# Two layers of a hybrid encoder trunk on one core: where the activation's hi and lo parts start in SBUF, relative to the weights'

## The chip, the cores and the metric

The kernel runs on one core of one Trainium2 chip. The time is device microseconds of one execution; the verdict compares medians of repeated runs of the kernel before and the kernel after on the same chip.

## The reference

Two layers on x of shape (1, 256, 1024), in float32. Each has three sub-layers of the form x <- LayerNorm(alpha x + f(x)): a SwiGLU feed-forward network (FFN) of width 2816, a mixer, and a second FFN.

```python
for l in range(DEPTH):
    x = _layernorm(DEEPNORM_ALPHA * x + FFN_RES * _swiglu(x, ffn1_w_in[l], ffn1_w_out[l]), ln1_g[l], ln1_b[l])
    mix = _hybrid_mixer(x, l, w_mix_in[l], ...)
    x = _layernorm(DEEPNORM_ALPHA * x + mix, ln2_g[l], ln2_b[l])
    x = _layernorm(DEEPNORM_ALPHA * x + FFN_RES * _swiglu(x, ffn2_w_in[l], ffn2_w_out[l]), ln3_g[l], ln3_b[l])
```

The mixer multiplies the normalised stream h with one wide input projection, whose columns feed three branches and their gates: A, differential attention; B, a chunked state-space scan (SSD) behind a short convolution; C, stick-breaking attention. Each branch's output is projected to 1024 columns, multiplied by its sigmoid gate, and summed, and one output projection follows.

## The kernel before

**Products in three passes.** Every float32 factor of the large products is split into a high part (rounded to the matmul's float32r) and a low part (the rest): on ScalarE the cast at line 91 writes `whi`, on VectorE the subtraction at line 92 writes `wlo`. For activations `split_act` (lines 126 and 127) does the same. A product is hi x hi, then two cross terms: three matmuls (`passes`).

**Weights.** They come from HBM in blocks of 1 MB through the SP queue into `raw` (two buffers, line 105), are split in halves of 128 x 1024 into `whi` and `wlo` (six buffers each), and are used once. TensorE gives the buffers back.

**Activations.** The stream x (256 tokens in two tiles of 128, t = 0 and 1) is kept transposed as `xT`: `xThi` and `xTlo`, each 8 slices (k) of 256 columns, so 8192 bytes of a partition. There are two ways of using it:
- *xT streamed.* `gemm_s` (line 133): the weights' 128 x 128 piece is stationary, 256 columns of `b[:, k, :]` stream. It serves the FFN's gate and up products (`part_s`), most of the mixer's projections (`block_s`) and the branch projections (`proj`, where b is the branch's output oA, oB or oC). A block of 256 weight columns is 2 x 8 x 3 = 48 matmuls.
- *xT stationary.* `block_a` (line 362, 512 weight columns stream) in the mixer and `part_a` (line 269, 256 columns) for the first tile of an FFN.

The FFN's middle parts `hhi` and `hlo` are stationary at line 302, under 512 streamed columns of the output weights: `whi`/`wlo`, or, for the last three tiles, `dhi`/`dlo`, which are kept until the LayerNorm of t = 0 is under way. The mixer's `mT` is stationary at line 724.

**Order.** The matmuls' order on TensorE is that of the program's planner; the order within a block is written out. At the end of a sub-layer the LayerNorm of t = 0 runs while the held matmuls of t = 1 go on, and the transposes (line 143) and `split_act` of each t build the next xT. In the mixer the scan's decay matrices come back through a DMA (line 457) to VectorE (line 489), ScalarE (line 493) and VectorE again (line 494), and line 500's matmuls use them.

**Where things lie.** A buffer starts where the one before it in its pool ends, rounded up to 32 bytes; pools stand one behind another, and the FFN's and the mixer's pool start at the same place. Counted from the declared sizes, in bytes modulo 512: `ident` 128, `xt`, `xThi`, `xTlo`, `raw`, `whi` and `wlo` 96; all large tiles of the FFN 288 (gb, sq, rawo, hhi, hlo, h, dhi, dlo); the mixer's slots 288, up to `cbm` at 352, and `t10` and `q3` at 384. The branch outputs use slots: oA in t6 and t7 (hi, lo), oB in t9 and t10, oC and later mT in t1 and t3.

Of the kernel before, what the change touches and what calls it, by code (L numbers as in the profile page):

```python
# [11 lines left out]
F32 = mybir.dt.float32  # L12
F32R = mybir.dt.float32r
# [7 lines left out]
P = 128  # L21
D = 1024
S = 256
L = 2
FF = 2816
KT = D // P
NT = S // P
EPS = 1e-5
ALPHA = (2 * L) ** 0.25
LAG = 2  # L30
HOLD = 3
OFF_QA, OFF_KA, OFF_VA, OFF_ZB, OFF_XBC, OFF_DTB, OFF_QC, OFF_KC, OFF_VC, OFF_G = (
    0, 1024, 2048, 3072, 4096, 5632, 5648, 6672, 7696, 8720)
NEG = -float(2 ** 100)
# [4 lines left out]
def hybrid_trunk(ctx: ExitStack, tc: tile.TileContext, x, ffn1_w_in, ffn1_w_out, ln1_g, ln1_b,  # L39
# [6 lines left out]
    const = ctx.enter_context(tc.tile_pool(name="const", bufs=1))  # L46
    keep = ctx.enter_context(tc.tile_pool(name="keep", bufs=1))
    wraw = ctx.enter_context(tc.tile_pool(name="wraw", bufs=2))
    wsp = ctx.enter_context(tc.tile_pool(name="wsp", bufs=6))
    sm = ctx.enter_context(tc.tile_pool(name="sm", bufs=2))  # L50
# [21 lines left out]

    ident = const.tile([P, P], F32, name="ident")
    make_identity(nc, ident)
    half_neg = const.tile([P, 8], F32, name="half_neg")
    dve.memset(half_neg, -0.5)


# [39 lines left out]
    def load_rows(w, k0, dst=None, raw=None):  # L118
        with tc.issue_after(dma[0]):
            return load(w, k0, 2, 0, 1024, dst, None, raw)  # L120
# [24 lines left out]
            split_act(xT[0][:, 4 * q:4 * q + 4, t * P:(t + 1) * P], xT[1][:, 4 * q:4 * q + 4, t * P:(t + 1) * P], pv)  # L145

    def new_xT():
        return (keep.tile([P, KT, S], F32R, name="xThi"), keep.tile([P, KT, S], F32R, name="xTlo"))

    def layernorm(t, accs, coef, gb, sq):  # L150
        st = sm.tile([P, 5], F32, name="st")
        for h in range(2):
            yh = xt[:, t, h * 512:(h + 1) * 512]
            dve.scalar_tensor_tensor(out=yh, in0=accs[h], scalar=coef / ALPHA, in1=yh, op0=ALU.mult, op1=ALU.add,  # L154
                                     accum_out=st[:, h:h + 1])
        dve.tensor_scalar(out=st[:, 4:5], in0=st[:, 0:1], scalar1=st[:, 1:2], scalar2=-1.0 / (D * math.sqrt(D)),
                          op0=ALU.add, op1=ALU.mult)
        dve.tensor_scalar(out=st[:, 2:3], in0=st[:, 0:1], scalar1=st[:, 1:2], scalar2=-1.0 / D, op0=ALU.add, op1=ALU.mult)
        act.activation(out=sq, in_=xt[:, t, :], func=AF.Square, bias=st[:, 4:5], scale=1.0 / math.sqrt(D),
                       accum_out=st[:, 3:4])  # L160
        rs = sm.tile([P, 1], F32, name="rs")
        for h in range(2):
            dve.scalar_tensor_tensor(out=accs[h], in0=xt[:, t, h * 512:(h + 1) * 512], scalar=st[:, 2:3],  # L163
                                     in1=gb[:, 0, h * 512:(h + 1) * 512], op0=ALU.add, op1=ALU.mult)
        dve.tensor_scalar(out=rs, in0=st[:, 3:4], scalar1=EPS / (ALPHA * ALPHA), scalar2=None, op0=ALU.add)
        pool.tensor_tensor(out=rs, in0=rs, in1=half_neg[:, 0:1], op=ALU.pow)
        for h in range(2):
            dve.scalar_tensor_tensor(out=xt[:, t, h * 512:(h + 1) * 512], in0=accs[h], scalar=rs,
                                     in1=gb[:, 1, h * 512:(h + 1) * 512], op0=ALU.mult, op1=ALU.add)
# [60 lines left out]
    def ffn(xT, w_in, w_out, g, b, l, pre, prefetch, fresh=False, last=False, tiles_a=1):  # L230
        NJ = FF // 256
        with tc.tile_pool(name="ffn", bufs=2, reuse_waits="tile") as fp:
# [4 lines left out]
            def new_raw():  # L237
                return fp.tile([P, 2048], F32, name="rawo")
# [4 lines left out]
            def held_pair():  # L243
                return (fp.tile([P, 2048], F32R, name="dhi", bufs=HOLD), fp.tile([P, 2048], F32R, name="dlo", bufs=HOLD))

# [62 lines left out]
            for j in range(tiles_a, NJ + LAG):  # L308
# [3 lines left out]
                if pj < 0:  # L312
                    continue
                if pj < NJ - HOLD:
                    wo = load_rows(w_out[l], 2 * pj, None, raws[pj] if pj < 2 and not fresh else new_raw())
# [15 lines left out]
            for t in range(NT):  # L331
                if t == 1:
                    for h in range(2):
                        for pj, wo in held:
                            out_mm(pj, hs[pj], wo, 1, (h,))
                layernorm(t, accs[t], 0.5, gb, sq)
                if last:
                    for h in range(2):
                        nc.sync.dma_start(out=out_v[:, t, 512 * h:512 * h + 512], in_=xt[:, t, 512 * h:512 * h + 512])
                else:  # L340
                    if xT2 is None:
                        xT2 = new_xT()
                    transposed(t, xT2)
# [3 lines left out]
    def mixer(xT, l, pre, prefetch, consts):  # L347
# [4 lines left out]
        with tc.tile_pool(name="mix", bufs=1, reuse_waits="tile") as mp:  # L352
            def slot(tag, shape, dt=F32):
                return mp.tile(shape, dt, name=tag, tag=tag)
# [11 lines left out]
            def block_s(c0, evac, w=wm):  # L366
# [3 lines left out]
                    gemm_s(ps[:, f * S:(f + 1) * S], ws, f * P, xT)  # L370
                evac(ps.rearrange("p (f c) -> p f c", c=S))

            zs = slot("t1", [P, NT, D])
            xs = slot("t2", [P, NT, D])
            xdt = slot("t3", [P, NT, D])
# [25 lines left out]
            for cc in range(6):  # L401
                def evac(ps, cc=cc):
                    pad = mp.tile([P, 768], F32, name="w3", bufs=4)[:, 0:2 * 259].rearrange("p (f c) -> p f c", c=259)
                    ac = mp.tile([P, 768], F32, name="w3", bufs=4)[:, 0:512].rearrange("p (f c) -> p f c", c=S)
                    dve.memset(pad[:, :, 0:3], 0.0)
                    act.copy(out=pad[:, :, 3:259], in_=ps)
                    for f in range(2):
                        c = 2 * cc + f
                        act.activation(out=ac[:, f, :], in_=ps[:, f, :], func=AF.Identity,
                                       scale=v[:, 36 + c:37 + c], bias=v[:, 48 + c:49 + c])  # L410
                        for i in range(3):
                            dve.scalar_tensor_tensor(out=ac[:, f, :], in0=pad[:, f, i:i + S],
                                                     scalar=v[:, 12 * i + c:12 * i + c + 1], in1=ac[:, f, :],
                                                     op0=ALU.mult, op1=ALU.add)
                    if cc >= 4:
                        last_silu[0] = act.activation(out=bcF[:, 2 * (cc - 4):2 * (cc - 4) + 2, :], in_=ac, func=AF.Silu).ins
                        return
                    act.activation(out=ac, in_=ac, func=AF.Silu)
                    pt = tp_tile()
                    for t in range(NT):  # L420
                        for f in range(2):
                            pe.transpose(out=pt[:, t * S + f * P:t * S + (f + 1) * P],
                                         in_=ac[:, f, t * P:(t + 1) * P], identity=ident)
                    act.copy(out=xs[:, :, cc * 256:(cc + 1) * 256], in_=pt.rearrange("p (t c) -> p t c", c=256))
# [57 lines left out]
                act.copy(out=cbm[:, g, 1, :], in_=pb[:, P:S])  # L482
                dve.tensor_mul(out=cbm[:, g, 2, :], in0=pb[:, S:S + P], in1=triu)

            ms = mp.tile([P, NT, 2], F32, name="ms")
            for c in range(NT):
                m = bcs[c]
                for h in range(16):
# [33 lines left out]
            for k2 in range(4):  # L522
                pt = tp_tile()
                for f in range(2):
                    k = 2 * k2 + f
# [87 lines left out]

            nl = bv[:, 48:49]
            oA = (slot("t6", [P, KT, S], F32R), slot("t7", [P, KT, S], F32R))
            ss = mp.tile([P, NT, 8], F32, name="ss")
            wT2 = slot("cbm", [P, 2, 384])
            for hq in range(4):
                po = tp_tile()
                pov = po.rearrange("p (t h e) -> p t h e", t=NT, h=2)  # L620
                for hi_ in range(2):
                    h = 2 * hq + hi_
# [135 lines left out]
            for t in range(NT):  # L758
                if t == 1:
                    for h in range(2):  # L760
                        for q in (1, 2, 3):
                            mix_out(q, wo[q], t, (h,))
                layernorm(t, accs[t], 0.5, gb, slot("xde", [P, D]))
                if xT2 is None:
                    xT2 = new_xT()
                transposed(t, xT2)
        return xT2, pre2

    def ffn_first(w_in, l, between=None):
        return lambda: (load_cols(w_in[l], 0, between), load_cols(w_in[l], FF))  # L770

    xT = new_xT()
    consts = []
    pre = ffn_first(ffn1_w_in, 0, lambda: load_x(0, 1))()
    for l in range(L):
        xT, pre = ffn(xT, ffn1_w_in, ffn1_w_out, ln1_g, ln1_b, l, pre, lambda: load_block(w_mix_in[l], OFF_ZB),
                      fresh=(l == 0))
        xT, pre = mixer(xT, l, pre, ffn_first(ffn2_w_in, l), consts[0])
        last = l == L - 1
        xT, pre = ffn(xT, ffn2_w_in, ffn2_w_out, ln3_g, ln3_b, l, pre, None if last else ffn_first(ffn1_w_in, l + 1), last=last)  # L780
# [37 lines left out]
```

## Time and profile before

| | us |
|---|---|
| median of 3 runs | 1632.81 (1632.53 to 1636.63) |
| the profiled execution | 1631.6 |
| its span, first to last instruction | 1629.8 |
| TensorE busy (matmuls) | 1607.9, 99% |
| VectorE busy | 984.4, 60% |
| ScalarE busy | 848.4, 52% |
| DMA | 283.55 MB, mean 174 GB/s |

How to read it: TensorE's matmuls overlap in the pipeline, so the mean of one is a latency. What one costs is the distance from its start to the start of the next, which the timeline gives. PE is TensorE's stream of matmuls, PEld its weight loads (one for each matmul); DVE is VectorE, ACT is ScalarE. In names of groups, out<-in, the second operand is the stationary one at line 133 (gm<-xThi,whi: xThi streams, whi is stationary), and so everywhere; t is any of the mixer's slots t1 to t10.

### The profile page before, as it was taken

To read this page: it belongs to the slowest core of one execution; us is meant where nothing else is said; L and a number is where in the kernel's file an instruction comes from. 1 tells how busy PE (TensorE), PEld (TensorE's weight loads), DVE (VectorE), ACT (ScalarE), POOL (GpSimd) and SP (SyncE) were. 2 spreads that over 40 slices of the span, in tenths; PEclk is the share of its full clock that TensorE was granted. 3 is DMA by queue.
4 is the path that set the end of the run, shared out by engine and by line. 5 is a ranking of instruction groups with operands and counts; after the bars stand their busy time and mean duration, and the time that the engine had idled before them with its cause. 6 is when DMAs were issued, how large, how long until landed. Compare 5 with 4: busy or idle time off the path is not lost.

```text
span 1629.8 us, 26930 instructions
## 1 busy us (share of the span) xinstructions
PE 1607.9 (99%) x11282; PEld 1481.9 (91%) x11282; DVE 984.4 (60%) x1510; ACT 848.4 (52%) x1285; POOL 17.6 (1%) x28
## 2 busy tenths in 40 slices
PE   8999999999999999999999999999999999999998
PEld 8999899988789998999899998998788999999997
DVE  5555657766585566454654465677575855565454
ACT  5544456468675444444444453654676755444451
POOL 0000000000000000000000000000000000000000
PEclk9999999999999999999999999999999999999999
DMA  8665445553434664566445662663443356645650
GB/s 284 196 218 197 157 155 163 181 174 104 155 105 159 229 231 133 183 213 219 159 157 205 204 229 86 188 199 131 156 134 127 129 181 217 197 155 182 232 195 38
DMA packets 222118, 283.55 MB, mean 174 GB/s; under 512 B 8659, under 2 KB 185645, under 8 KB 221997
## 3 DMA queue, kind: packets, MB, share of 16 engines
q1 hardware_dynamic: 213676, 277.61, 51.1%
q10 hardware_dynamic: 8320, 4.23, 0.9%
q8 instruction: 88, 1.44, 0.4%
q14 instruction: 34, 0.27, 0.0%
HBM read 280.74 MB, written 1.08 MB: 173 GB/s over the span
## 4 chain that ended last, share of the span: by engine, by line
PE 95%; DMA 2%; DVE 2%; ACT 1%; issue 0%; SPq 0%; POOL 0%; DVEq 0%; POOLq 0%; ACTq 0%
PE gm L133 53%; PE at L302 15%; PE gm L362 14%; PE gm L269 3%; PE at L724 2%; DMA t<-acd 2%; PE at L627 1%; PE at L578 1%; PE at L500 1%; PE at L570 1%; PE at L548 1%; DMA raw<-in_ffn_w_in_dram 1%; PE tp L607 0%; DVE wlo L92 0%; DVE at L163 0%; DVE xt L154 0%
## 5 line engine op out<-in xcount | busy, mean ns | idle before, releaser
L92 DVE TENSOR_TENSOR wlo<-raw,whi 128x1024 fp32r<-128x1024 f32 x412 | 501.1, 1222 | 376.6 <-ACT whi L91 368.1
L91 ACT CAST whi<-raw 128x1024 fp32r<-128x1024 f32 x412 | 428.9, 1049 | 406.9 <-PE gm L133 241.8
L133 PE MATMUL gm<-xThi,whi 128*128 128x256 f32 x2112 | 600.2, 284 | 0.0
L133 PE MATMUL gm<-xTlo,whi 128*128 128x256 f32 x2112 | 599.8, 284 | 0.0
L133 PE MATMUL gm<-xThi,wlo 128*128 128x256 f32 x2112 | 599.4, 284 | 0.0
L133 PEld LDWEIGHTS gm<-xThi,whi 128*128 128x128 f32 x2112 | 403.7, 191 | 3.5 <-issue 1.8
L133 PEld LDWEIGHTS gm<-xTlo,whi 128*128 128x128 f32 x2112 | 403.6, 191 | 3.2 <-issue 1.6
L133 PEld LDWEIGHTS gm<-xThi,wlo 128*128 128x128 f32 x2112 | 403.7, 191 | 1.8 <-issue 1.8
L133 PE MATMUL gm<-t,whi 128*128 128x256 f32 x768 | 137.9, 281 | 0.0
L362 PE MATMUL gm<-whi,xThi 128*128 128x512 f32 x320 | 127.8, 399 | 1.1 <-ACT xThi L126 1.1
L92 DVE TENSOR_TENSOR wlo<-rawo,whi 128x1024 fp32r<-128x1024 f32 x68 | 82.9, 1225 | 73.8 <-ACT whi L91 73.8
L362 PE MATMUL gm<-whi,xTlo 128*128 128x512 f32 x320 | 126.3, 396 | 0.0
L362 PE MATMUL gm<-wlo,xThi 128*128 128x512 f32 x320 | 126.3, 395 | 0.0
L133 PEld LDWEIGHTS gm<-t,whi 128*128 128x128 f32 x768 | 117.2, 188 | 2.7 <-issue 2.7
L91 ACT CAST whi<-rawo 128x1024 fp32r<-128x1024 f32 x68 | 71.0, 1049 | 79.3 <-PE at L302 66.1
L133 PE MATMUL gm<-t,wlo 128*128 128x256 f32 x384 | 107.4, 280 | 0.0
L302 PE MATMUL at<-wlo,hhi 128*128 128x512 f32 x256 | 79.5, 392 | 0.0
L302 PE MATMUL at<-whi,hlo 128*128 128x512 f32 x256 | 79.5, 392 | 0.0
L302 PE MATMUL at<-whi,hhi 128*128 128x512 f32 x256 | 79.4, 391 | 0.0
L362 PEld LDWEIGHTS gm<-whi,xThi 128*128 128x128 f32 x320 | 60.1, 188 | 14.0 <-ACT xThi L126 2.0
L133 PEld LDWEIGHTS gm<-t,wlo 128*128 128x128 f32 x384 | 72.4, 188 | 0.0
L362 PEld LDWEIGHTS gm<-whi,xTlo 128*128 128x128 f32 x320 | 60.1, 188 | 12.9 <-DVE xTlo L127 0.9
(235 smaller groups left out, 1862.6 us busy)
## 6 DMA issues: line engine op xcount, KB each, us to landing
raw<-in_w_mix_in_dram SPq DMA_DIRECT2D x92, 1024.0 KB, 5.2
raw<-in_ffn_w_in_dram SPq DMA_DIRECT2D x85, 1024.0 KB, 5.1
rawo<-in_ffn_w_out_dram SPq DMA_DIRECT2D x44, 1024.0 KB, 7.2
raw<-in_w_branch_dram SPq DMA_DIRECT2D x24, 1024.0 KB, 5.4
raw<-in_w_mix_out_dram SPq DMA_DIRECT2D x8, 1024.0 KB, 5.7
t<-acd ACTq DMA_DIRECT2D x4, 1024.0 KB
rawo<-in_ffn_w_in_dram SPq DMA_DIRECT2D x2, 1024.0 KB
gb<-in_ln_g_dram SPq DMA_DIRECT2D x4, 512.0 KB
```

Source lines behind the costliest of these rows:

```text
L91: act.copy(out=hi, in_=src)
L92: dve.tensor_sub(out=lo, in0=src, in1=hi.bitcast(F32))
L133: pe.matmul(out=ps_out, lhsT=a[:, f:f + n], rhs=b[:, k, :], start=first, stop=(k == KT - 1 and i == 2))
L269: pe.matmul(out=ps[:, u * 256:(u + 1) * 256], lhsT=a[:, k, t * P:(t + 1) * P], rhs=c, start=first, stop=(k == KT - 1 and i == 2))
L302: pe.matmul(out=accs[t][h], lhsT=a[:, f, t * P:(t + 1) * P], rhs=c[:, h * 512:(h + 1) * 512], start=(j == 0 and f == 0 and i == 0), stop=( ...
L362: pe.matmul(out=ps, lhsT=a[:, k, t * P:(t + 1) * P], rhs=c, start=(k == 0 and i == 0), stop=(k == KT - 1 and i == 2))
L500: pe.matmul(out=py[:, 64 * h:64 * h + 64], lhsT=m[:, hh, :], rhs=xdt[:, c, 64 * hh:64 * hh + 64], start=True, stop=True)
L548: pe.matmul(out=pz[h][:, 0:S], lhsT=kcT[r, hp, 0:P], rhs=qcT[r, hp, :], start=True, stop=False, skip_group_check=True)
L570: pe.matmul(out=pz[h][:, 0:384], lhsT=trin, rhs=part[:, hs], start=False, stop=False, skip_group_check=True)
L578: pe.matmul(out=pz[c0][64 * h:64 * h + 64, 384:512], lhsT=vct[:, k, 64 * hh:64 * hh + 64], rhs=sp[:, 384 * h + c1:384 * h + c1 + P], start ...
L627: pe.matmul(out=pm[m][:, c:c + n], lhsT=qaT[r, h, t * P:(t + 1) * P], rhs=kaT[r, h, 0:n], start=True, stop=True, skip_group_check=True)
L724: pe.matmul(out=accs[t][h], lhsT=a[:, k, t * P:(t + 1) * P], rhs=c[:, h * 512:(h + 1) * 512], start=(k == 0 and i == 0), stop=(k == KT - 1 ...
```

## The change

It changes where buffers start, and no instruction's work:
- `half_neg` has 112 columns in place of 8 (448 bytes for 32). All that lies behind it moves by 416 bytes, so `xt`, `raw`, `whi` and `wlo` start at 0 modulo 512.
- `xThi` and `xTlo` are slices of tiles with 128 columns more; the slice starts at column 48, 192 bytes into the tile, so at 192 modulo 512.
- `rs` has 48 columns for 1 (two buffers of 192 bytes for 32), so that the FFN's and the mixer's pools start at 0: `hhi`, `hlo`, `dhi`, `dlo` and `rawo` lie at 0.
- In the mixer `ss` is declared first, with 192 bytes, so the slots that follow lie at 192; `ms` has 448 bytes for 32, so that `t10` lies at 192 too.

```diff
+APART = 48
-    half_neg = const.tile([P, 8], F32, name="half_neg")
+    half_neg = const.tile([P, 112], F32, name="half_neg")
 ...
     def new_xT():
-        return (keep.tile([P, KT, S], F32R, name="xThi"), keep.tile([P, KT, S], F32R, name="xTlo"))
+        def part(name):
+            whole = keep.tile([P, KT * S + 128], F32R, name=name)
+            return whole[:, APART:APART + KT * S].rearrange("p (k c) -> p k c", c=S)
+
+        return part("xThi"), part("xTlo")
 ...
-        rs = sm.tile([P, 1], F32, name="rs")
+        rs = sm.tile([P, 48], F32, name="rs")[:, 0:1]
 ...
+            ss = mp.tile([P, APART], F32, name="ss")[:, 0:2 * 8].rearrange("p (t h) -> p t h", h=8)
             zs = slot("t1", [P, NT, D])
 ...
-            ms = mp.tile([P, NT, 2], F32, name="ms")
+            ms = mp.tile([P, 112], F32, name="ms")[:, 0:4].rearrange("p (c g) -> p c g", g=2)
 ...
-            ss = mp.tile([P, NT, 8], F32, name="ss")
```

## Rows read from the trace of the kernel before

**Rows 1.** The page: span; busy time of TensorE; the chain that ended last, by line

```profile
span 1629.8 us, 26930 instructions
PE 1607.9 (99%) x11282; PEld 1481.9 (91%) x11282; DVE 984.4 (60%) x1510; ACT 848.4 (52%) x1285; POOL 17.6 (1%) x28
...
PE gm L133 53%; PE at L302 15%; PE gm L362 14%; PE gm L269 3%; PE at L724 2%; DMA t<-acd 2%; PE at L627 1%; PE at L578 1%; PE at L500 1%; PE at L570 1%; PE at L548 1%; DMA raw<-in_ffn_w_in_dram 1%; PE tp L607 0%; DVE wlo L92 0%; DVE at L163 0%; DVE xt L154 0%
```

**Rows 2.** Waits of TensorE's matmuls: us in total, times, longest

```profile
PE tp L143 <- DMA xt<-in_x_dram: 5.1, 2, 4.2
PE gm L269 <- DVE xTlo L127: 3.7, 4, 1.6
```

**Rows 3.** Groups by line: shape, count | busy us, mean ns | idle before

```profile
L133 PE MATMUL gm<-xThi,whi 128*128 128x256 f32 x2112 | 600.2, 284 | 0.0
...
L133 PE MATMUL gm<-t,whi 128*128 128x256 f32 x768 | 137.9, 281 | 0.0
L362 PE MATMUL gm<-whi,xThi 128*128 128x512 f32 x320 | 127.8, 399 | 1.1 <-ACT xThi L126 1.1
...
L133 PE MATMUL gm<-t,wlo 128*128 128x256 f32 x384 | 107.4, 280 | 0.0
L302 PE MATMUL at<-wlo,hhi 128*128 128x512 f32 x256 | 79.5, 392 | 0.0
```

**Rows 4.** Timeline, first and last of 96 matmuls with xT: start, us, what

```profile
102.62 0.28 PE L133 MATMUL gm<-xThi,whi 128*128 128x256 f32 x1
...
114.02 0.28 PE L133 MATMUL gm<-xThi,wlo 128*128 128x256 f32 x1
```

**Rows 5.** Timeline, a block of 48 with oA: first, fourth, last

```profile
559.02 0.40 PE L133 MATMUL gm<-t,whi 128*128 128x256 f32 x2
...
559.38 0.39 PE L133 MATMUL gm<-t,whi 128*128 128x256 f32 x2
...
564.37 0.28 PE L133 MATMUL gm<-t,wlo 128*128 128x256 f32 x1
```

**Rows 6.** Windows xT, oA, oC, oB, held, L362, L302: PE/PEld/DVE/ACT/POOL busy, clock, DMA share, GB/s

```profile
102.62:114.02 11.40, 11.40 (x97) 11.40 (x96) 4.97 (x5) 4.69 (x5) 0.00 (x0) 1.00 0.79 290
559.02:564.37 5.35, 5.35 (x50) 5.35 (x48) 4.47 (x4) 3.79 (x5) 0.00 (x0) 1.00 0.57 182
547.82:553.17 5.35, 5.35 (x50) 5.35 (x48) 2.29 (x3) 2.84 (x4) 0.00 (x0) 1.00 0.59 198
536.41:541.95 5.54, 5.54 (x49) 5.54 (x48) 2.30 (x3) 2.84 (x4) 0.00 (x0) 1.00 0.69 235
182.17:198.29 16.12, 16.12 (x73) 13.34 (x72) 8.52 (x17) 2.92 (x4) 0.56 (x1) 1.00 0.32 96
207.31:223.21 15.90, 15.90 (x71) 13.14 (x70) 7.81 (x9) 7.61 (x9) 0.00 (x0) 1.00 0.42 132
97.12:102.39 5.27, 5.27 (x26) 4.33 (x25) 3.33 (x4) 2.58 (x3) 0.00 (x0) 1.00 0.43 140
```

**Rows 7.** Timeline of line 269: the first and the last of 23 matmuls

```profile
18.82 0.28 PE L269 MATMUL gm<-whi,xThi 128*128 128x256 f32 x1
...
21.46 0.28 PE L269 MATMUL gm<-wlo,xThi 128*128 128x256 f32 x1
```

**Rows 8.** Line 91 (ScalarE's splits): its idle time until, in us, times

```profile
  PE gm L133: 252.4, 185
...
  DMA raw<-in_w_mix_in_dram: 24.6, 12
```

**Rows 9.** Timeline around line 500: layer 1 (TensorE), then layer 0 (VectorE, TensorE)

```profile
1082.64 0.36 PE L133 MATMUL gm<-xThi,wlo 128*128 128x256 f32 x1
...
1105.53 0.66 PE L500 MATMUL at<-t,t 128*128 128x64 f32 x4 [1.06 <-DVE t L494]
...
298.05 1.22 DVE L494 TENSOR_TENSOR t<-t,cbm 128x1024 f32<-128x1024 f32 x1
...
299.31 0.88 PE L500 MATMUL at<-t,t 128*128 128x64 f32 x6
```

## The prediction

> **What bounds the kernel now.** I read the page first. TensorE is busy for 99% of the span, and the chain that ended last is TensorE's almost throughout, 53% of the span at line 133 alone [rows 1]. Then the waits of TensorE: the longest totals are 5.1 us for the first load of x and 3.7 us at the start of an FFN [rows 2]. So nothing feeds this kernel too late; TensorE's own pace is the time, and the question is what sets that pace.
>
> The groups by line tell the counts: line 133 has 3 x 2112 matmuls of 256 columns that stream xThi or xTlo, and 768 + 384 that stream a branch output (t is a slot: oA in t6/t7, oB in t9/t10, oC in t1/t3); line 362 has 3 x 320 of 512 columns with xT stationary, line 302 768 with the FFN's middle parts stationary under whi/wlo [rows 3]. The means there (284, 281, 399 ns) are latencies that overlap, so they are no price. The price of one is the distance between two starts, which I take from the timeline and from windows that run from the first start to the last.
> - xT streamed: 96 starts in 11.40 us, so 11.40 / 95 = 120.0 ns [rows 4, 6].
> - oA streamed, the same line, shape and weights: 48 starts in 5.35 us, 5.35 / 47 = 113.8 ns [rows 5, 6]. The first three after the switch still take 120 ns (559.02 to 559.38), the next 44 take 4.99 / 44 = 113.4 [rows 5]. oC gives the same 5.35 us [rows 6].
> - oB streamed: 5.54 / 47 = 117.9 ns [rows 6].
> - 512 columns: FFN's middle parts under whi/wlo 5.27 / 23 = 229.1 ns, the same parts under the held dhi/dlo 16.12 / 71 = 227.0, xT under whi/wlo (line 362) 15.90 / 70 = 227.1 [rows 6].
>
> All of these stretches run at a granted clock of 1.00, the 2.4 GHz level [rows 6], so the clock doesn't separate them. Nor does the other engines' work: oA's stretch is the one with the busiest VectorE (4.47 of 5.35 us) and is among the fast ones [rows 6]. What separates them is where the operands lie. Counted modulo 512 bytes, from the declared sizes, the weights lie at 96. xT lies at 96 too (distance 0: 120.0). oA and oC lie at 288 (streamed part 192 past the stationary one: 113.8). oB is mixed, one part 192 past, the other 288 (117.9). For 512 columns distance 0 gives 227 (xT under whi, hhi under dhi), and a stationary part that lies 192 past the streamed one gives 229.1. That two tiles at 96 and two at 288 give the same 227 says that the distance counts, not the place.
>
> **The change part by part.**
> - xT streamed at line 133 goes from distance 0 to 192, which is what oA and oC have. 6336 x (120.0 - 113.8) = 39.3 us less. All of it lies on the path, since TensorE is the chain. Bounds: 113.4 if no lead-in is left (41.8 us), 117.9 if it only gets as far as oB (13.3 us, a rival below). I take 113.8, the mean of whole blocks.
> - oB's second part goes from 288 to 192 past: 384 x (117.9 - 113.8) = 1.6 us less. oA, oC and mT keep their distance: nothing.
> - The FFN's middle parts go from 192 past whi/wlo to 0: 768 x (229.1 - 227.0) = 1.6 us less. Under dhi/dlo they stay at 0.
> - xT stationary at line 362 goes the other way, from 0 to 192 past the streamed weights: 960 x 2.1 = 2.0 us more, by line 302's row. Bounds: 0, and twice that.
> - xT stationary at line 269 does the same with 256 columns. It runs at 120.0 now (22 intervals in 2.64 us) [rows 7]; no row has this distance with 256 columns. From below the 6.2 ns of line 133 (384 of them: 2.4 us less), from above the 2.1 ns of line 302 (0.8 us more). I take +0.8, the row with the same sign of the distance.
> - The supply of weights must keep the new pace. ScalarE's splits at line 91 stand idle for 252.4 us in 185 waits until line 133's matmuls give a buffer back, and for 24.6 us in 12 waits for the largest load's data [rows 8]: they run ahead. A block of 48 matmuls eats 1 MB in 5.8 us and would in 5.5; in the xT window the DMA moved 290 GB/s [rows 6] against the 192 GB/s that this asks. Nothing added. If that cover were gone, each block would lose at most the 0.3 us it gains.
> - One cover does end. Before line 500 TensorE works through line 133 from 1082.64 us on, while VectorE waits for a DMA of its own; then TensorE waits 1.06 us for line 494 and goes on at 1105.53 [rows 9]. These 21.8 us of cover (1105.53 - 1.06 - 1082.64) shrink by 6.2 / 120 = 1.1 us and the chain over the DMA doesn't. In layer 0 the matmuls come 0.04 us after line 494 ends (298.05 + 1.22 against 299.31) [rows 9], so there it bares the same 1.1: 2.2 us given back. The other waits of TensorE [rows 2] stand behind LayerNorms, whose cover is line 302, 269 and 362, not 133.
> - The padding itself: 104 more columns of one memset and wider tiles for scalars, which change no instruction of a loop. `ss` is merely declared earlier. The mixer's slots now reach 192 bytes into the next FFN buffer, so a slot can wait for one more tile of the phase before. The early ones wait for something later already: t1 now covers a corner of sq too, but it waits for gb, which the LayerNorm reads after sq. Nothing.
>
> Sum: -39.3 - 1.6 - 1.6 + 2.0 + 0.8 + 2.2 = -37.5 us, so a span of 1629.8 - 37.5 = 1592.3. The profiled execution took 1631.6 us, 1.8 more than its span, and the median of the runs is 1632.81, another 1.2: 1592.3 + 3.0 = 1595.3 us, 0.977 of before.
>
> One shape and one clock show 120.0 and 113.8 ns by the place of the streamed part alone [rows 4, 5]. The Trainium skill speaks against that: SBUF — State Buffer, section "Who interferes with whom", gives TensorE two independent read ports, one for the streamed operand and one for weight loads, and knows a single rule of contention, the port pair that VectorE and GpSimd share. By that rule the place of xT could not matter and the sum would be 0; by the rows it is -37.5.
>
> **The rivals.**
> - *Distance isn't the cause.* oA and oC could be faster for another reason, say because they lie above the weights in the partition and xT below. For: only two pairs of tiles show 113.8. Against: oB lies above as well and takes 117.9, and hhi under dhi (both above) and xT under whi (one below) take the same 227 [rows 6]. Then line 133 stays at 120.0 and the whole is 1632.8. Chance 0.03. The rule of the Trainium skill named above would be this case.
> - *Half of it.* xT could settle in oB's pattern (117.9), since it is streamed in every stage and interleaved with more: 6336 x 2.1 = 13.3 us in place of 39.3, the lost cover 0.8 in place of 2.2: 1632.8 - 13.3 - 1.6 - 1.6 + 2.8 + 0.8 = 1620. Or, with the same result, xT as a slice of a flat tile makes the halves t = 0 and t = 1 one to the planner, so that at five stage starts the 24 matmuls of t = 0 (24 x 229 ns = 5.5 us) no longer cover the other half's LayerNorm: 1595 + 27 = 1622. Against: the slices are written by the same strided pattern as before. Together 0.05.
> - *Better.* Streamed and stationary parts now start on multiples of 64 bytes, where before all started 32 past one. No row shows such a pair. If this took the interval from 113.8 as far again as the distance did (107.6), 39 us more would go: 1556. Chance 0.03.
> - *Slower: the sign is wrong.* The stationary part 192 past the streamed one is line 302's distance, the slowest row (229.1). If the buffers don't land where the sizes say, and xT gets that side of the weights, line 133 pays 2.1 ns more in place of 6.2 less: 6336 x 2.1 = 13.3, and with line 302 back at 227.0 the time is 1632.8 + 13.3 - 1.6 = 1645. It decides from 0.8 ns above 120.0 on (4.9 us over 6336). Against: sizes and the rounding to 32 bytes are all that places a buffer here. Chance 0.03.
>
> **How the numbers follow.** The forecast of 1595 has 0.86. Its own range: best terms, line 133 at 113.4 (-41.8), line 362 at 0, line 269 at -2.4, no cover lost: -41.8 - 3.2 - 2.4 = -47.4, so 1585. Worst: line 362 twice as dear (+2.0), the lost cover doubled and as much again for waits that no row shows (+6), the lead-in of 120 ns more often (+3): 1606. 1585 to 1606 holds well over 8 in 10 and leaves out the four rivals (0.14). A measurement of this kernel can tell about 0.3%, 4.9 us, from no change: faster 0.86 + 0.05 + 0.03 = 0.94, the same 0.03, slower 0.03.
>
> **What would show it.** Starts at line 133 with xT 113 to 114 ns apart, in the FFN as in the mixer, would show the main term right; 118 or 120 would show it wrong. The middle parts at line 302 should come at 227, xT at lines 362 and 269 at some 229 and 122. Line 500 should wait longer, about 1 us in layer 0 and 2 in layer 1. What would make the prediction wrong is a new wait of TensorE at line 133 on VectorE's wlo (then the supply was closer than the waits say) or on xTlo at the stage starts (then the flat tiles cost cover).

## The result: 1.0% faster, where 2.3% was forecast

The kernel after takes 1618.65 us (median of 4 runs, 1610.39 to 1620.61), beside 1633.03 for the kernel before on the same chip: ratio 0.9898, 95% interval 0.986 to 0.9935. Four more runs in a later series gave 1611.29 us and 0.9882 [0.9865, 0.9898]; the runs of after differ by how long TensorE's clock was granted at half (1610.39 us with a mean granted clock of 0.998, 1620.61 with 0.992). The forecast was 1595 us, 0.977. The order and the number of the instructions are the same. The lines moved: 133 is now 135, 269 is 275, 302 is 308, 362 is 368, 494 and 500 are 501 and 507.

The page of the profile after, with the lines that answer to [rows 1] and [rows 3]:

```profile
span 1615.6 us, 26930 instructions
PE 1591.5 (99%) x11282; PEld 1467.2 (91%) x11282; DVE 984.7 (61%) x1510; ACT 848.4 (53%) x1285; POOL 17.6 (1%) x28
...
L135 PE MATMUL gm<-xThi,whi 128*128 128x256 f32 x2112 | 595.1, 282 | 0.0
...
L135 PE MATMUL gm<-t,whi 128*128 128x256 f32 x768 | 138.7, 282 | 0.0
```

TensorE is still busy for 99%. Its means hardly moved (284 to 282 ns), as a latency would. The pace stands in the windows. Those after, in the columns of [rows 6]: xT in the first FFN of layer 0, xT in the mixer, oA, oB, the middle parts (line 308), line 368:

```profile
101.20:112.38 11.18, 11.18 (x96) 11.18 (x95) 4.95 (x5) 4.70 (x5) 0.00 (x0) 1.00 0.79 298
222.78:236.03 13.25, 13.25 (x119) 13.25 (x118) 8.72 (x14) 7.91 (x13) 0.00 (x0) 1.00 0.73 234
552.44:557.98 5.54, 5.54 (x50) 5.54 (x48) 4.56 (x4) 3.75 (x5) 0.00 (x0) 1.00 0.58 192
529.83:535.36 5.53, 5.53 (x49) 5.53 (x48) 2.33 (x3) 2.83 (x4) 0.00 (x0) 1.00 0.72 240
112.50:117.72 5.22, 5.22 (x26) 4.33 (x24) 3.35 (x4) 2.57 (x3) 0.00 (x0) 1.00 0.47 146
204.68:220.72 16.04, 16.04 (x71) 13.16 (x70) 8.08 (x9) 7.59 (x9) 0.00 (x0) 1.00 0.42 131
```

Each window runs from a first start to a last, and its count can hold a neighbour that reaches in. xT's 96 starts in the FFN are 11.18 / 95 = 117.7 ns apart (120.0 before), its 118 starts in the mixer 13.25 / 117 = 113.2. **One line, one distance, one clock, and two paces.** And oA, whose distance the change didn't touch, went from 113.8 to 5.54 / 47 = 117.9. The middle parts take 5.22 / 23 = 227.0 (229.1 before), line 368 takes 16.04 / 70 = 229.1 (227.1 before).

TensorE's waits, and line 93 (ScalarE's splits, line 91 before), answering to [rows 2] and [rows 8]:

```profile
PE tp L145 <- DMA xt<-in_x_dram: 5.4, 2, 4.6
PE gm L275 <- DVE xTlo L129: 3.7, 4, 1.6
PE at L507 <- DVE t L501: 3.1, 2, 1.6
```

```profile
  PE gm L135: 240.9, 183
...
  DMA raw<-in_w_mix_in_dram: 22.5, 12
```

Line 507 now waits for VectorE's line 501 in both layers, 3.1 us in all; before, the wait was 1.06 us in layer 1 [rows 9] and next to nothing in layer 0. The supply of weights kept up: the splits still wait 240.9 us for TensorE and 22.5 us for the largest load.

**The sum of the two profiled executions.** From start to start of TensorE's matmuls, added up by line (waits in a row of their own), in us:

| | forecast | measured |
|---|---|---|
| line 133/135 with xT | -39.3 | -19.1 |
| the same line with oA, oB, oC | -1.6 | +0.7 |
| line 302/308, middle parts | -1.6 | -2.0 |
| line 362/368, xT stationary under 512 columns | +2.0 | +1.1 |
| line 269/275, xT stationary under 256 columns | +0.8 | +2.3 |
| waits for line 494/501 at line 500/507 | +2.2 | +1.9 |
| everything else | 0 | +0.9 |
| span | -37.5 | -14.2 |

Of the 23.3 us that are missing, 20.2 are xT's pace at line 135 and 2.3 the branch outputs'; the rest nets to 0.8. The clock is in these rows too. The windows show the stretches after where it was granted at half (0.50, the 1.2 GHz level), start and end of the span left out, and behind them the only one of before:

```profile
619.45:622.80 3.35, 3.35 (x18) 3.35 (x17) 2.07 (x4) 0.00 (x0) 0.56 (x1) 0.50 0.76 267
1093.90:1104.10 10.20, 10.20 (x50) 10.20 (x50) 10.20 (x15) 3.18 (x5) 0.00 (x0) 0.50 0.32 104
1421.56:1424.95 3.39, 3.39 (x19) 3.39 (x18) 2.62 (x5) 0.00 (x0) 0.56 (x1) 0.50 0.88 299
```

```profile
1107.40:1114.20 6.80, 6.80 (x34) 6.80 (x33) 6.80 (x10) 1.83 (x3) 0.00 (x0) 0.50 0.41 133
```

That is 16.9 us at half clock, against 6.8 before. Line 275's matmuls come some 213 ns apart in such a stretch, so nearly half of it is lost, and the difference is some 5 us (an estimate). Some 3 us of it fall on line 275, the rest on lines 507 and 135. So line 275 lost 2.3 us though its matmuls otherwise come at 117.8 ns in place of 120.0.

### The profile page after: what moved, and what is told of

Read it like the earlier page. It is cut to its first block, busy times and chain, and to the rows that moved or that the text cites. A ratio compares the mean times of both kernels' runs of the same rounds, so it can differ in the third digit from the quotient of the medians.

```text
span 1615.6 us, 26930 instructions
## 1 busy us (share of the span) xinstructions
PE 1591.5 (99%) x11282; PEld 1467.2 (91%) x11282; DVE 984.7 (61%) x1510; ACT 848.4 (53%) x1285; POOL 17.6 (1%) x28
## 4 chain that ended last, share of the span: by engine, by line
PE 95%; DVE 2%; DMA 2%; ACT 1%; issue 0%; POOL 0%; DVEq 0%; POOLq 0%; ACTq 0%
PE gm L135 52%; PE at L308 15%; PE gm L368 14%; PE gm L275 3%; PE at L730 2%; DMA t<-acd 2%; PE at L633 1%; PE at L507 1%; PE at L585 1%; PE at L577 1%; PE at L555 1%; PE tp L614 0%; DVE wlo L94 0%; DVE at L169 0%; DVE xt L160 0%; PE tp L145 0%
## 5 line engine op out<-in xcount | busy, mean ns | idle before, releaser
L135 PEld LDWEIGHTS gm<-xThi,whi 128*128 128x128 f32 x2112 | 398.4, 189 | 3.4 <-issue 1.8
L135 PEld LDWEIGHTS gm<-xTlo,whi 128*128 128x128 f32 x2112 | 397.9, 188 | 3.0 <-issue 1.6
```

What stands on the lines that cost most here:

```text
L135: pe.matmul(out=ps_out, lhsT=a[:, f:f + n], rhs=b[:, k, :], start=first, stop=(k == KT - 1 and i == 2))
```

## The experiments

**Theory and rivals after the result.** At a distance of 192 bytes there are two paces, and something other than the place picks one (theory). Or the paces depend on other things than the distance: the DMA's load, VectorE's work, the absolute place (rival 1). Or the second edit, the middle parts at distance 0 from the weights, has to do with it (rival 2). Where paces are given without a row, they are the mean distance of the last 24 starts of a block of 48, so without its lead-in; for 512 columns that of the last 12 of 24.

**1. The distance by itself** (`d_sweep`). A kernel of matmuls alone, with line 135's block and passes, the weights at 0 modulo 512 and X at 0, 32, ... 480:

```python
for f in range(2):
    for k in range(8):
        for i, (a, b) in enumerate(passes(ws[k], x)):
            pe.matmul(out=ps[:, 256 * f:256 * f + 256], lhsT=a[:, 128 * f:128 * f + 128], rhs=b[:, k % 4, :], ...)
```

> A kernel of matmuls alone: 16 places of a streamed part X, 0 to 480 bytes past the weights' 512-byte grid in steps of 32, and at each place 48 matmuls of line 133's three-pass pattern (256 columns) twice, once straight after 12 matmuls of 512 columns and once after 4 transposes; then X stationary under 256 and under 512 columns of the weights. Nothing of the network is computed. Theory 1 (the distance alone sets the pace): one interval for each distance, whatever ran before: about 120 ns at 0 and about 113.5 at 192. Theory 2 (at one distance there are two paces, and what ran before picks one): at 192 the block after the wide matmuls runs at about 118 and the block after the transposes at about 113.5. For X stationary under 512 columns: 227 at 0, 229 at 192.

Measured, ns: a block after 12 matmuls of 512 columns, the same after 4 transposes, and X as the stationary part under 256 and under 512 columns.

| X past the weights | after 512 columns | after transposes | stationary, 256 | stationary, 512 |
|---|---|---|---|---|
| 0 | 120.0 | 120.0 | 120.0 | 226.7 |
| 32 | 116.7 | 116.7 | 118.3 | 233.3 |
| 64 | 117.8 | 117.8 | 117.8 | 233.3 |
| 96 | 120.0 | 120.0 | 117.3 | 234.3 |
| 128 | 120.0 | 118.7 | 118.7 | 232.8 |
| 160 | 118.5 | 118.7 | 120.0 | 233.3 |
| 192 | 117.8 | 113.3 | 117.8 | 228.9 |
| 224 | 118.3 | 118.3 | 116.7 | 233.3 |

From 256 to 480 the table repeats to the digit. The windows of this kernel, in the columns used above: distance 0 after 512 columns; 192 after 512 columns and after transposes; the same two blocks at 448:

```profile
55.97:61.61 5.64, 5.64 (x49) 5.63 (x47) 0.00 (x0) 0.00 (x0) 0.00 (x0) 1.00 0.01 3
...
216.31:221.85 5.54, 5.54 (x49) 5.53 (x47) 0.00 (x0) 0.00 (x0) 0.00 (x0) 1.00 0.02 3
222.37:227.75 5.38, 5.38 (x49) 5.38 (x48) 0.00 (x0) 0.00 (x0) 0.00 (x0) 1.00 0.00 0
429.58:435.12 5.54, 5.54 (x49) 5.54 (x47) 0.00 (x0) 0.00 (x0) 0.00 (x0) 1.00 0.01 3
435.64:441.02 5.38, 5.38 (x50) 5.38 (x48) 0.00 (x0) 0.00 (x0) 0.00 (x0) 1.00 0.00 0
```

VectorE and ScalarE do nothing here and the DMA next to nothing, and both paces are there. Only X moves in this kernel, so by itself it can't tell distance from place; the kernel before can. There oA at 288 with the weights at 96 (192 past) settled at 113.4, while X at 288 with the weights at 0 takes 116.7; and hhi at 288 under dhi at 288 took 227.0, while X at 288 (32 in the table) under weights at 0 takes 233.3. So rival 1 falls: the distance modulo 256 bytes sets the pace, and at 192 what TensorE ran before picks one of two. The Trainium skill's rule that the prediction weighed (SBUF — State Buffer, section "Who interferes with whom", two independent read ports for TensorE) doesn't describe this: the place alone moves 256 columns between 113.3 and 120.0 ns and 512 columns between 226.7 and 234.3.

**2. xT back at distance 0** (`xt_at_0`), all else as after:

```diff
-            return whole[:, APART:APART + KT * S].rearrange("p (k c) -> p k c", c=S)
+            return whole[:, 0:KT * S].rearrange("p (k c) -> p k c", c=S)
```

> The kernel after with one part undone: the slices of xThi and xTlo start at byte 0 of their tiles, on the weights' grid, as before; the FFN's middle parts and all slots stay as in the kernel after. If the distance of xT is what brings the gain, line 133 with xT goes back to 120 ns, lines 362 and 269 lose their 1 to 2 us, and the time comes to about 1631. If the gain came from the other parts, it stays near 1618.

Measured 1628.29 us (10 runs), ratio 0.9979 [0.9964, 0.9993]. The windows of 96 matmuls with xT in the FFN, of the middle parts, and of oA:

```profile
103.53:114.92 11.39, 11.39 (x97) 11.39 (x95) 4.99 (x5) 4.69 (x5) 0.00 (x0) 1.00 0.78 292
115.04:120.28 5.24, 5.24 (x26) 4.32 (x24) 3.32 (x4) 2.57 (x3) 0.00 (x0) 1.00 0.45 135
559.38:564.72 5.34, 5.34 (x49) 5.34 (x48) 4.53 (x4) 3.79 (x5) 0.00 (x0) 1.00 0.57 189
```

11.39 / 95 = 119.9 ns: the pace of before. So xT's place brings most of the gain. The other edits by themselves are worth 1632.3 - 1628.29 = 4.0 us here (1.1 to 5.9 by the interval), forecast 3.2; by line it is 1.0 us at line 308 and 1.1 for the branch outputs. And this run shows in the whole kernel what picks oA's pace: the edit leaves oA where it is in the kernel after, and with xT back at distance 0 the same block takes 5.34 / 47 = 113.6 ns again, in place of 117.9.

**3. The middle parts back at 192** (`mid_at_192`), xT as after:

```diff
-        rs = sm.tile([P, 48], F32, name="rs")[:, 0:1]
+        rs = sm.tile([P, 1], F32, name="rs")
...
-            ss = mp.tile([P, APART], F32, name="ss")[:, 0:2 * 8].rearrange("p (t h) -> p t h", h=8)
+            ss = mp.tile([P, 128], F32, name="ss")[:, 0:2 * 8].rearrange("p (t h) -> p t h", h=8)
```

> The kernel after with the other part undone: the FFN's tiles (hhi, hlo, dhi, dlo, rawo) lie 192 bytes past the weights' grid again, xT and the mixer's slots stay 192 past it. Theory 1 (distance alone): line 302 back at 229 ns, 1.6 us more than the kernel after, line 133 unchanged. Theory 2 (what ran before picks the pace): the FFN's gate and up blocks follow line 302's matmuls, so a change of their distance can move line 133's pace in the FFN, now 117.8 ns: to 113.5 it would take 16 us off, to 120 it would add 9.

Measured 1609.74 us, ratio 0.9864 [0.9829, 0.99]: no slower without the second edit. Windows of the first FFN (line 135, line 308) and of the second (line 308, line 135):

```profile
101.30:112.09 10.79, 10.79 (x97) 10.79 (x95) 4.86 (x5) 4.70 (x5) 0.00 (x0) 1.00 0.76 289
112.20:117.47 5.27, 5.27 (x26) 4.33 (x25) 3.42 (x4) 2.58 (x3) 0.00 (x0) 1.00 0.54 170
...
653.23:658.52 5.29, 5.29 (x26) 4.32 (x25) 3.35 (x4) 2.59 (x3) 0.00 (x0) 1.00 0.50 167
658.74:669.93 11.19, 11.19 (x96) 11.18 (x95) 4.94 (x5) 4.69 (x5) 0.00 (x0) 1.00 0.54 193
```

The first FFN now streams xT at 10.79 / 95 = 113.6, from 101 us on (before that it changes between the paces), the second at 11.19 / 95 = 117.8; the fourth goes with the first, the third with the second. After, all four are at 117.8 but for some 35 matmuls at their start. Beside the second profiled execution of after (experiment 7), line 135 takes 6.1 us less in all (884.5 to 878.4) and line 308 takes 2.3 us more (239.2 to 241.5). Rival 2 holds in part: the edit saves at line 308 what was forecast and gives back more at line 135. By the two ratios alone it can't be told, since their intervals overlap; the two lines tell it.

**4. What picks the pace** (`kicks`). Matmuls alone, X at 192; each series is a block after 512-column matmuls, then four times an interruption and a block:

```python
for kick in (lambda: tr(1), ..., lambda: some(1, 64), lambda: some(1, 128), ...):
    wide()
    block(at(192))
    for _ in range(4):
        kick()
        block(at(192))
```

> Matmuls alone, nothing of the network: X streamed 192 bytes past the weights' grid, blocks of 48 matmuls of line 133's pattern. Twelve series; each is 12 matmuls of 512 columns, a block, and then four times a small interruption and a block. The interruptions: 1, 2, 3 or 4 float32 transposes; one matmul of 64, 128, 384 or 512 columns; two of 128; one or two of 256 columns with 32 stationary columns; eight of 64. Theory 1 (distance alone): every block of every series at the same pace. Theory 2 (two paces at one distance, picked by what ran before): the first block of each series at 117.8 ns, and after an interruption 113.3 or 117.8, the same for the same interruption; some interruption always leads to 113.3 or turns one into the other.

The first block after the wide ones is at 117.8 in all twelve series. The four after an interruption:

| interruption | paces of the next four blocks, ns |
|---|---|
| 1 matmul of 64 columns, or of 384, or of 256 with 32 stationary columns | 113.3, 113.3, 113.3, 113.3 |
| 1 matmul of 512; 3 transposes | 117.8, 117.8, 117.8, 117.8 |
| 2 of 128 | 117.8, 113.3, 113.3, 113.3 |
| 1 of 128; 1 transpose | 117.8, 113.3, 117.8, 117.8 |
| 2 transposes | 117.8, 113.3, 117.8, 113.3 |
| 4 transposes; 8 of 64; 2 of 256 with 32 stationary | 113.3, 117.8, 113.3, 117.8 |

Windows of the 64-column series (first block and the next two), then of the 512-column series:

```profile
183.94:189.47 5.53, 5.53 (x48) 5.53 (x47) 0.00 (x0) 0.00 (x0) 0.00 (x0) 1.00 0.00 0
189.62:195.05 5.43, 5.43 (x51) 5.43 (x49) 0.00 (x0) 0.00 (x0) 0.00 (x0) 1.00 0.00 0
195.19:200.60 5.41, 5.41 (x50) 5.41 (x49) 0.00 (x0) 0.00 (x0) 0.00 (x0) 1.00 0.01 3
...
276.68:282.21 5.53, 5.53 (x48) 5.53 (x47) 0.00 (x0) 0.00 (x0) 0.00 (x0) 1.00 0.00 0
282.56:288.09 5.53, 5.53 (x48) 5.53 (x47) 0.00 (x0) 0.00 (x0) 0.00 (x0) 1.00 0.00 0
```

5.43 us holds a lead-in of five slower starts (200, 118, 122, 116 and 114 ns) before the pace of 113.3. Behind the lead-in the pace is kept to the block's end. The same interruption can leave it, lift it or flip it in turn, so it acts on a state that the block before left; a single 64-column matmul sets the better one here, from either pace.

**5. Is 192 the best place?** (`fine_sweep`): X from 160 to 256 in steps of 4, one block after 512 columns, two after transposes.

> Matmuls alone: X streamed 160 to 256 bytes past the weights' grid in steps of 4, at each place a block of 48 after 12 wide matmuls and two more blocks, each after 2 transposes. In the coarse sweep 192 gave 117.8 after the wide ones and 113.3 after 4 transposes, its neighbours 160 and 224 about 118.5 both times. Theory 2 wants a range around 192 in which both paces occur; a place with 113.3 in all three blocks would be a better place than 192. Theory 1 would show one pace for each place.

Only 192 shows 113.3 at all (117.8, 113.3, 117.8). All other places lie between 117.0 and 123.3 ns, 188 at 118.9 and 196 at 122. What ran before counts at some of them too: 180, 204, 244 and 252 differ by 2 to 4 ns between their three blocks (204: 118.3, 120.0, 117.8), as 128 does by 1.3 ns in experiment 1. No place has 113.3 in all three blocks.

**6. Other transposes in the kernel** (`four_transposes`): the pairs of transposes of t = 1 are issued twice.

```diff
-                        for f in range(2):
+                        for f in (range(2) if t == 0 else (0, 1, 0, 1)):
```

> The kernel after, and in part_a of each FFN the two transposes of the second token half are issued twice into the same place (2 x 4 more matmuls of 128 columns in all, about 1 us). Theory 2: in the kernel after this pair stands between a stretch of line 133 at 113.3 ns and one at 118.3, and the rest of the FFN keeps 117.8; a second pair may turn it back, and then the four FFNs (some 1000 matmuls each) run at 113.6 and the time falls by up to 4 x 4.3 = 17 us, to about 1601. Theory 1: nothing but the 1 us.

Measured 1612.74 us, ratio 0.9895 [0.9878, 0.9911]: no gain. Windows of the second FFN, right behind the transposes and one block later:

```profile
638.15:654.91 16.76, 16.76 (x150) 16.76 (x149) 8.73 (x10) 9.16 (x11) 0.00 (x0) 1.00 0.77 279
660.48:671.67 11.19, 11.19 (x97) 11.19 (x95) 4.96 (x5) 4.70 (x5) 0.00 (x0) 1.00 0.55 198
```

In the second FFN, and likewise in the fourth, the transposes pick the pace of what follows (148 starts, 16.76 / 147 = 114.0 in place of 118.3), but after the next line 308 it is 11.19 / 95 = 117.8 again; the other two FFNs run nearly as after. So line 308 with its middle parts at distance 0 seems to put the pace back, which experiment 10 takes by itself.

**7 to 9. A settling matmul before every block** (`after_again`, `settle_after`, `settle_before`): one matmul of 64 columns ahead of each of 92 blocks, in the kernel after and in the kernel before, beside after once more.

```diff
+    def settle(ps, w):
+        pe.matmul(out=ps[:, 0:64], lhsT=w[0][0][:, 0:P], rhs=w[0][0][:, 0:64], start=True, stop=True)
...
+                settle(pg, wg)
...
+                settle(ps, ws)
```

> The kernel after once more, beside the two with the settling matmul on one chip. About 1611 to 1619; the spread goes with the granted clock (0.991 to 0.998 in its first runs).

> The kernel after, and before each block of part_s and block_s one matmul of 64 columns (weights against weights) into the place that the block then overwrites: 92 more matmuls, some 60 ns each, 5.5 us. In the series of interruptions this kind led every block to 113.3 ns and kept it there. Theory 2 (two paces, picked by what ran before): the FFNs go from 117.8 to 113.5 (about 3900 matmuls, 16.5 us), the gates and branch projections in the mixers' second half as well (about 1000, 4.3 us), line 133 with xT has one pace, and the time falls by some 15 us, to about 1600. Theory 1 (the distance alone, and 117.8 in the kernel for another reason): 5 us slower than the kernel after.

> The kernel before (distance 0) with the same 92 settling matmuls. At distance 0 every block of the sweeps ran at 120.0, whatever stood before it: so both theories expect 5 us more than the kernel before, about 1638. If it gets faster, the settling matmul does something else than picking between the two paces of distance 192.

| | us | ratio to before |
|---|---|---|
| after, again | 1611.29 (1609.64 to 1612.73) | 0.9882 [0.9865, 0.9898] |
| after with settling | 1606.37 (1604.57 to 1612.12) | 0.9855 [0.9834, 0.9876] |
| before with settling | 1641.02 (1640.56 to 1641.56) | 1.0061 [1.0046, 1.0076] |

An FFN block of `settle_after`:

```profile
100.46:111.33 10.87, 10.87 (x97) 10.87 (x96) 4.88 (x5) 4.71 (x5) 0.00 (x0) 1.00 0.78 296
```

10.87 / 95 = 114.4 with the lead-in, 113.3 behind it, and so in all four FFNs but for a stretch at their start. At distance 0 the same matmuls change no pace (120.0) and cost 1641.02 - 1632.21 = 8.8 us, so some 96 ns each, with the slower starts behind them, where I had expected 60. If they cost the same at 192 (not measured apart), the net gain of 1611.29 - 1606.37 = 4.9 us is 13.7 us of pace less 8.8.

**10. What line 308 does to the pace** (`mid_sweep`). Matmuls alone: a block at 192, line 308's pattern with the middle parts at 0 to 224, a block at 192; twice from either pace. Line 308's pace is that of its last 20 starts.

> Matmuls alone: line 302's pattern (24 matmuls of 512 columns, middle parts stationary) with the middle parts 0 to 224 bytes past the weights in steps of 32, twice from a block at 113.3 and twice from one at 117.8 (X streamed 192 past), each followed by such a block. Theory 2 by the two kernels: with the middle parts at 0 the block that follows runs at 117.8, or keeps the pace that was; at 192 a block that was at 113.3 comes back at 113.3. Line 302 itself 226.7 at 0, 229 to 230 at 192.

| middle parts at | line 308's pace, ns | the block after it |
|---|---|---|
| 0 | 226.7 | 117.8, from either pace |
| 32 | 233.2 | from 113.3: 113.3; from 117.8: 117.8 after the first pattern, 113.3 after the second |
| 64 | 233.3 | the other pace |
| 96 | 234.3 | 113.3, from either |
| 128 | 232.6 | 113.3, from either |
| 160 | 233.2 | 113.3, from either |
| 192 | 228.8 from 113.3, 229.2 from 117.8 | the pace it had |
| 224 | 233.3 | 117.8 |

Windows up to the next block's first start, 24 matmuls each: middle parts at 0 from 113.3, then at 192 from 113.3 and from 117.8:

```profile
61.72:67.17 5.45, 5.45 (x26) 4.51 (x25) 0.00 (x0) 0.00 (x0) 0.00 (x0) 1.00 0.00 0
...
427.97:433.46 5.49, 5.49 (x26) 4.51 (x25) 0.00 (x0) 0.00 (x0) 0.00 (x0) 1.00 0.00 0
...
458.28:463.80 5.52, 5.52 (x27) 4.52 (x26) 0.00 (x0) 0.00 (x0) 0.00 (x0) 1.00 0.00 0
```

This is the second edit's price. With the middle parts at distance 0, line 308 is the fastest there is (226.7) and leaves every following block in the slower pace. At 192 it costs 2.1 ns more a matmul and keeps what it finds. No place is fast itself and sets 113.3.

**11. Settle once, and keep it** (`settle_once`): the layout of `mid_at_192`, and a settling matmul only where an FFN's third tile or a gate begins (10 in all).

```diff
+                if j == 2:
+                    settle(pg, wg)
...
-            def block_s(c0, evac, w=wm):
+            def block_s(c0, evac, w=wm, kick=False):
...
-                block_s(OFF_G + 1024 * r + 256 * dp, evac)
+                block_s(OFF_G + 1024 * r + 256 * dp, evac, kick=(dp == (3 if r else 0)))
```

> The layout with the middle parts at 192, where line 302 keeps the pace that it finds, and 10 settling matmuls in all: one in each FFN at the third tile, behind the part_a transposes, and three in each mixer's gates. About 1 us of them. Theory 2: the two FFNs that ran at 117.8 with the middle parts at 192 go to 113.5 (2 x 950 x 4.3 = 8 us), the mixers' last third too (4 us): from about 1609 to about 1598, faster than the kernel after and than 92 settling matmuls. Theory 1 (the distance alone): no different from the layout with the middle parts at 192, plus 1 us.

Measured 1601.43 us (1596.37 to 1606.47, 5 runs), ratio 0.9811 [0.9784, 0.9838]: the lowest median of all, and an interval below those of before and of after (it just overlaps those of `mid_at_192` and of after with settling). The second FFN, at 117.8 in `mid_at_192`:

```profile
660.54:671.32 10.78, 10.78 (x96) 10.78 (x95) 4.85 (x5) 4.70 (x5) 0.00 (x0) 1.00 0.54 198
```

10.78 / 95 = 113.5. Three of the four FFNs hold it; the first lost it at 84 to 96 us, where transposes of constants come in between. Line 135 takes 870.8 us in all, against 887.8 and 884.5 in the two profiled executions of after, and 904.2 at line 133 before.

**12. Why before showed only the better pace** (`from_zero`): blocks in turn at distance 192, 0, 192, 0, 192, mixed (192 and 288), 192, mixed.

> Matmuls alone, six times the same series: 12 wide matmuls, then blocks of 48 with X streamed at 192, 0, 192, 0, 192, then with one part at 192 and the other at 288, 192, and the mixed one again. This is what the kernel before did with oA and oC between xT at distance 0, and with oB. Theory 2, if it also explains the rows that misled the prediction: the first block at 117.8, those at 0 at 120.0, and the blocks at 192 that follow a block at 0 come at 113.3; the mixed ones at about 118. If the blocks at 192 after 0 stay at 117.8, oA's 113.8 in the kernel before had another cause.

The windows of the first four blocks of the first series:

```profile
56.34:61.88 5.54, 5.54 (x49) 5.54 (x47) 0.00 (x0) 0.00 (x0) 0.00 (x0) 1.00 0.02 3
61.99:67.64 5.65, 5.65 (x50) 5.65 (x49) 0.00 (x0) 0.00 (x0) 0.00 (x0) 1.00 0.00 0
67.75:73.10 5.35, 5.35 (x50) 5.35 (x49) 0.00 (x0) 0.00 (x0) 0.00 (x0) 1.00 0.01 3
73.21:78.85 5.64, 5.64 (x50) 5.64 (x49) 0.00 (x0) 0.00 (x0) 0.00 (x0) 1.00 0.00 0
```

The block at 192 takes 5.54 us behind 512 columns and 5.35 us behind a block at distance 0, in all six series alike. 5.35 us is to the digit what oA and oC took [rows 6]: they came behind xT at distance 0. The mixed blocks ran at 119.8 to 120.0, where some 118 had been expected; they stood behind blocks at 192, while oB stood behind xT at 0.

## Why the prediction was wrong, step by step

- **The step that failed is the first term:** "6336 x (120.0 - 113.8)", which took 113.8 as the property of a distance. At 192 bytes there are two paces, 113.3 and 117.8, and before showed one of them only because its blocks with oA and oC stood behind blocks at distance 0 (experiment 12, and oA in experiment 2). The change moved those neighbours too, so the very rows that carried the term lost their pace: oA went from 113.8 to 117.9. Measured, xT gained 19.1 us, or 3.0 ns on average for 6.2.
- **The hint stood in the rows.** "The first three after the switch still take 120 ns" was read as a lead-in to be averaged. It showed that the block before reaches into this one, and a rival "the neighbour sets the pace" was missing.
- **The middle parts at distance 0 were sized right and judged wrong.** Line 308 gained 2.0 us (forecast 1.6). That it also sets the pace of the xT blocks behind it is a cost that the prediction had no term for: some 6 us at line 135 by experiment 3. All four FFNs sit at 117.8 with it, two of the four without it.
- **oB's term** (-1.6) failed with the first one. Behind xT at distance 0 it holds: in `xt_at_0`, with both of oB's parts at 192, the branch outputs gain 1.1 us. Behind xT at 192 they lost 0.7. Why oB took 117.9 before, where mixed blocks alone took 120 behind others, stays open.
- **Right in cause:** the distance moves the pace (the rival "Distance isn't the cause" falls by experiments 1 and 2), the sign of it, line 368 (+1.1, bounds 0 and 4.0), the supply of weights, and the cover lost at line 500/507 (+1.9 for +2.2; only +0.9 in the second profiled execution). Line 275 is at 117.8 in place of 120.0, the other sign than the +0.8 taken; 2.4 us less was its lower bound. The clock hid that.
- **The rival "Half of it"** gave 1620, beside 1618.65 measured. That the two are so near is luck: 1618.65 holds the clock's loss, the second series gave 1611.29, and xT gained 19.1 us where this rival has 13.3. It named xT settling at 117.9, which is where the FFNs sit, but for oB's mixed distances and interleaving. With distance, interleaving and DMA unchanged, one 64-column matmul moves a block from 117.8 to 113.3, so its reason was another.
- **What was forecast can be had, though not by place alone:** `settle_once` at 1601.43 lies in the forecast's own range (1585 to 1606).

Open: what inside TensorE or its reads holds the two paces. The runs show paces, their period of 256 bytes and what switches them, no cause. Why the first part of the mixer takes 113.3 after line 368 and its last part 117.8 was not traced to one instruction.

## To carry to other kernels

A pace read from a few blocks is the pace of those blocks behind those neighbours: before a row is multiplied by 6336, look at what ran ahead of it, and whether the change moves that too. Where matmuls alone set the time, measure a layout's pace in a small kernel behind each kind of predecessor that the real one has. And cost an edit by what it does to the next block as well as to its own.

## What the runs showed of the hardware

- The distance between streamed and stationary operand, modulo 256 bytes, sets the pace of these matmuls (128 x 128 stationary, new for each) in a full pipeline at a granted clock of 1.00 (2.4 GHz). In steps of 32 bytes, 256 columns take 116.7 to 120.0 ns at seven places and 113.3 or 117.8 at 192, by what ran before; 512 columns take 226.7 at 0, 228.9 at 192, 232.6 to 234.3 elsewhere.
- One 64-column matmul between two blocks sets the 113.3 at 192; at distance 0 it changes no pace, and costs some 96 ns.
- The granted clock fell to 0.50 for 3.4 to 10.2 us inside a kernel whose TensorE is busy for 99%. Two of the falls after come at the start of an FFN, one at line 507, behind waits of at most 1.6 us. The waits at the FFNs' starts stood in before as well [rows 2], where the clock didn't fall; before's one fall came behind its wait of 1.06 us at line 500. Layer 0's wait of 1.5 us at line 507 was followed by none. After's second profiled execution (span 1607.9) had one such stretch. Why it falls in some executions stays open.
